# First layer's experts: gather evictions after both halves' matmuls, slot matrices a pair ahead, another order in the last pair's second product

## The chip, the cores and the metric

The program runs on 1 core of one Trainium2 chip, as one launch. The metric is the device time of that core in microseconds (us), the median of several runs. Engine names are those of the profile: PE is TensorE (PEld its weight loads), DVE is VectorE, ACT is ScalarE, POOL is GpSimd, SP is SyncE, which here only issues DMAs.

## What is computed

Two blocks, one after the other, on 512 latent tokens and 256 context tokens of width 1024. The first block has two layers: a mixer (a state-space scan in layer 0, attention in layer 1), then a mixture of experts in which each of 16 experts picks its own tokens. The change lies in layer 0's experts, which serve both token sets:

```python
def moe_ec(h, router_w, w1, w3, w2):
    cap = EC_CAPACITY * T // N_EXPERTS          # 64 latent, 32 context tokens an expert
    aff = jax.nn.softmax(einsum('btd,de->bte', h, router_w))
    gate, idx = lax.top_k(jnp.swapaxes(aff, 1, 2), cap)
    xg = h[bidx, idx]
    a = jnp.einsum('becd,edf->becf', xg, w1)
    g = jnp.einsum('becd,edf->becf', xg, w3)
    y = jnp.einsum('becf,efd->becd', jax.nn.silu(a) * g, w2)
    y = y * gate[..., None]
    return jnp.zeros_like(h).at[bidx, idx].add(y)
```

The second block (convolution, recurrence, pooling, sparse attention, memory attention, a gated feed-forward) follows and isn't touched.

## The kernel before, in words

`Kern.moe` (lines 1073 to 1186) does layer 0's experts, two at a time: 8 pairs. `big` is the latent set (residual `xT`), `small` the context set (residual `cT`). For a pair it forms `moe_w1` and `moe_w3` products (`pa`, `ca` and `pg`, `cg`), takes silu(a)·g on ACT and DVE, turns the three results with transposes (`flip`, banks `tp`), and forms the `moe_w2` product (`py`, `cy`). In a product the selected tokens are the stationary side and 1 MB weight tiles (`wm`, and `raw` in halves) stream past; `cy`, the context part, is interleaved with `py`, the latent part: 24 steps of four matmuls. Weights come through a ring of nine tiles (`Ring`), issued by SP in order as tiles come free.

The **gather**, `Router.quad` (line 328), makes the selected rows `xg` of four latent experts (eight context ones) as one-hot matmuls: for each of 4 PSUM banks, two halves of 8 matmuls (`xrh`, `xrl` over 4 token tiles), and behind each half its eviction, on DVE (line 349) for the first and on ACT (line 347) for the second. `gates` (line 351) follows with 16 small matmuls. Layer 0 gathers before pair 0 (banks `x`, `c`) and, in pairs 1, 3 and 5, after the flips (banks `s`). The same `quad` is called for the context set (lines 682 and 957) and for layer 1's experts (lines 1066 and 1206).

The **scatter** adds pair `pr`'s result `last` to the residuals in pair `pr+1`, between flips and `moe_w2`: `slots` makes one-hot slot matrices (`sp` matmul into PSUM, then `is_equal` on DVE: `ohT` for big, two `ohS` for small), `scatter_big` multiplies and adds on DVE (line 1139), `scatter_small` scales on ACT (`scc`, line 1148) and adds on POOL (line 1149). The last pair's scatter stands behind the loop.

What sets the order: within `moe` the order of TensorE's instructions is the program's (`manual_schedule` for PE); those of the other engines, and all outside `moe`, are put in order at build time by a planner that works with its own time estimates. Each engine then runs its list in order. Dependencies inside PSUM are kept by whole banks: while one engine reads a bank, no other instruction on it starts. Tags name banks through `Slots.MAP` (line 95): `x` is 6, 7; `s` rotates over 6, 0, 7, 1; `a` is 0, 1; `c` is 4, 5; `g` is 2, 3.

Behind `moe`, `attention` starts on the finished residuals: `rms_pe` squares the eight tiles of `xT` on ACT (`sq`, two buffers) and sums them on PE (`rmsps`); ACT makes `rs`; then the products with the first three weight tiles begin, which ACT casts (`whi`, line 443) and POOL splits (`wlo`, line 444).

Of the kernel before, what the change touches and what calls it, by code (L numbers as in the profile page):

```python
# [14 lines left out]
F32R = mybir.dt.float32r  # L15
BF16 = mybir.dt.bfloat16
AF = mybir.ActivationFunctionType
ALU = mybir.AluOpType
# [4 lines left out]
P = 128  # L23
D = 1024
KT = 8
S = 512
C = 256
# [181 lines left out]
class Router:  # L209
# [118 lines left out]
    def quad(self, q, pp, *tags):  # L328

        K, nc, nt, cap, ne = self.K, self.K.nc, self.nt, self.cap, self.ne  # L330
        oh = self.oh = self.rp.tile([P, nt, 256], F32R, name=self.nm + "oh", tag="oh", bufs=1)
        for t in range(nt):
            nc.vector.tensor_tensor(oh[:, t, :].rearrange("p (e j) -> p e j", e=ne),
                                    K.mk["iof"][:, 0:cap].unsqueeze(1).to_broadcast([P, ne, cap]),
                                    self.slot[:, t, q * ne:(q + 1) * ne].unsqueeze(2).to_broadcast([P, ne, cap]), op=ALU.is_equal)
        xg = self.xg[q] = self.xgp.tile([P, KT, 256], F32, name=self.nm + "xg", tag=self.nm + "xg", bufs=self.nq)
        for k2 in range(KT // 2):
            ps = pp.tile([P, 2, 256], F32, name="gth", tag=tags[k2 % len(tags)])
            for z2 in range(2):
                k = 2 * k2 + z2  # L340
                for t in range(nt):
                    for z, r in enumerate((self.rh, self.rl)):
                        nc.tensor.matmul(ps[:, z2, :], r[:, t, k * P:(k + 1) * P], oh[:, t, :],  # L343
                                         start=(t == 0 and z == 0), stop=(t == nt - 1 and z == 1))
                A, sh = K.A2[self.layer][:, self.c, k:k + 1], K.mod(self.layer, 3, self.c, k)
                if z2:
                    nc.scalar.activation(xg[:, k, :], ps[:, z2, :], AF.Identity, scale=A, bias=sh)
                else:
                    nc.vector.tensor_scalar(xg[:, k, :], ps[:, z2, :], A, sh, op0=ALU.mult, op1=ALU.add)
# [28 lines left out]
class Kern:  # L378
# [694 lines left out]
    def moe(self, st, layer, R, nw2):  # L1073
# [3 lines left out]
        nc, tc = self.nc, self.tc  # L1077
        ep = self.pool(st, "moe_e")
        big, small = R
# [4 lines left out]
        ring = Ring(self, rings, 3)  # L1084
        pp = self.pp
        sel, iop = self.mk["sel"], self.mk["iop"]
        bank = lambda nm, tag: pp.tile([P, 512], F32, name=nm, tag=tag)

        def product(nm, pr, lb, ls, pb, pc):

            for q in range(4):
                w = [ring.tile(self.I[nm][layer, 2 * pr + e, q * 256:(q + 1) * 256, :]) for e in range(2)]
                steps = [(a, z) for a in range(2) for z in (0, 1, 2)] if q < 3 else [(a, z) for z in (0, 1, 2) for a in range(2)]
                for a, z in steps:
                    k = 2 * q + a
                    f = dict(start=(k == 0), stop=(k == KT - 1))
                    for e in range(2):
                        for h in range(2):
                            o = 64 * e + 32 * h
                            if z < 2:  # L1100
                                nc.tensor.matmul(pb[z][o:o + 32, :], lb(k, e)[:, 32 * h:32 * h + 32], w[e][a][:, z * 512:(z + 1) * 512], tile_position=(0, o), **f)  # L1101
                            else:
                                nc.tensor.matmul(pc[o:o + 32, :], ls(k, e), w[e][a][:, h * 512:(h + 1) * 512], tile_position=(0, o), **f)  # L1103

        def silu(src):
            t = ep.tile([P, 512], F32, name="ac", tag="ac", bufs=3)
# [1 line left out]
            return t  # L1108

        def flip(src, dst):  # L1110
            tp = bank("tp", "x")
            for j in range(4):
                nc.tensor.transpose(tp[:, j * P:(j + 1) * P], src[:, j * P:(j + 1) * P], self.ident)
            nc.scalar.copy(dst[:, 0:2, :].rearrange("p a b -> p (a b)"), tp[:, 0:256])
            nc.vector.tensor_copy(dst[:, 2:4, :].rearrange("p a b -> p (a b)"), tp[:, 256:512])

        def scaled(src, gate):
            hi = ep.tile([P, 512], F32R, name="yhi", tag="yhi", bufs=3)
            lo = ep.tile([P, 512], F32R, name="ylo", tag="ylo", bufs=3)
            nc.scalar.activation(hi, src, AF.Copy, scale=gate)  # L1120
            nc.vector.scalar_tensor_tensor(lo, src, gate, hi.bitcast(F32), op0=ALU.mult, op1=ALU.subtract)
            return hi, lo

        def slots(s, pr, cols):
            n = s.n
            ps = bank("sp", "s")
            nc.tensor.matmul(ps[:, 0:n], sel[:, pr].rearrange("p e j -> p (e j)"), s.slotT, start=True, stop=True)
            r = []
            for cix in cols:
                t = ep.tile([P, 512], F32R, name="ohT", tag="ohT", bufs=2)[:, 0:n] if n == S else ep.tile([P, C], F32R, name="ohS", tag="ohS", bufs=2)  # L1130
                nc.vector.tensor_scalar(t, ps[:, 0:n], iop[:, cix:cix + 1], None, op0=ALU.is_equal)
                r.append(t)
            return r

        def scatter_big(y, o, k, kk):
            ps = bank("sc", "s")
            for z in range(2):
                nc.tensor.matmul(ps, y[z][:, kk * P:(kk + 1) * P], o, start=(z == 0), stop=(z == 1))
            nc.vector.scalar_tensor_tensor(big.res[:, k, :], ps, self.mod(layer, 5, 0, k), big.res[:, k, :], op0=ALU.mult, op1=ALU.add)

        def scatter_small(y, o, k, kk):
            ps = bank("scs", "s")
            for j in range(2):
                for z in range(2):
                    nc.tensor.matmul(ps[:, j * C:(j + 1) * C], y[z][:, (kk + j) * P:(kk + j + 1) * P], o, start=(j == 0 and z == 0), stop=(j == 1 and z == 1))
            for j in range(2):
                t = ep.tile([P, C], F32, name="scc", tag="scc", bufs=2)
                nc.scalar.activation(t, ps[:, j * C:(j + 1) * C], AF.Copy, scale=self.mod(layer, 5, 1, k + j))  # L1148
                nc.gpsimd.tensor_tensor(small.res[:, k + j, :], small.res[:, k + j, :], t, op=ALU.add)  # L1149

        def scatter(pr, yb, yc):

            ob, oc = slots(big, pr, (0,))[0], slots(small, pr, (1, 2))
            for i in range(4):
                for j in range(2):
                    k = 2 * i + j
                    scatter_big(yb[k // 4], ob, k, k % 4)
                scatter_small(yc, oc[i // 2], 2 * i, 2 * (i % 2))

        with tc.manual_schedule(engines={mybir.EngineType.PE}):  # L1160
            big.quad(0, pp, "x", "c")
            big.gates(0, pp, "x")
            last = None
            for pr in range(8):
                e0 = 2 * pr
                pa, ca = [bank("pa", "a") for _ in range(2)], bank("ca", "c")
                product("moe_w1", pr, lambda k, e: big.rows(k, e0 + e), lambda k, e: small.rows(k, e0 + e), pa, ca)
                ac = [silu(t) for t in (*pa, ca)]
                pg, cg = [bank("pg", "g") for _ in range(2)], bank("cg", "c")
                product("moe_w3", pr, lambda k, e: big.rows(k, e0 + e), lambda k, e: small.rows(k, e0 + e), pg, cg)  # L1170
                for t, g in zip(ac, (*pg, cg)):
                    nc.vector.tensor_tensor(t, t, g, op=ALU.mult)  # L1172
                aT = ep.tile([P, KT, P], F32, name="aT", tag="aT", bufs=1)
                cT = ep.tile([P, 4, P], F32, name="cT", tag="cT", bufs=1)
                for t, o in zip(ac, (aT[:, 0:4, :], aT[:, 4:8, :], cT)):
                    flip(t, o)
                if pr % 2 and pr < 7:
                    big.quad(pr // 2 + 1, pp, "s")
                    big.gates(pr // 2 + 1, pp, "s")
                if last:  # L1180
                    scatter(*last)
                py, cy = [bank("py", "g") for _ in range(2)], bank("cy", "c")
                product("moe_w2", pr, lambda k, e: aT[:, k, 64 * e:64 * e + 64],
                        lambda k, e: cT[:, k % 4, 64 * e + 32 * (k // 4):64 * e + 32 * (k // 4) + 32], py, cy)
                last = (pr, [scaled(t, big.gate[:, pr:pr + 1]) for t in py], scaled(cy, small.gate[:, pr:pr + 1]))
            scatter(*last)

    def moe_last(self, st, R, head):

# [1263 lines left out]
```

## Time and profile before

| | us |
|---|---|
| median of 3 runs | 3378.2 |
| the three runs | 3374.7, 3378.2, 3380.14 |
| the profiled execution | 3374.78 |
| its span | 3373.1 |
| PE / DVE / ACT / POOL busy in the span | 94% / 49% / 35% / 29% |
| mean granted TensorE clock | 0.975 |

Layer 0's experts take about 932 to 1574 us of the span. The times of the sum below are those of the profiled execution, which ran 3.4 us under the median. A granted clock of 1.00 is TensorE's 2.4 GHz, 0.50 its 1.2 GHz.

### The profile page before, as it was taken

What the parts mean: (1) busy time and instruction counts of PE and PEld (TensorE: products, weight loads), DVE (VectorE), ACT (ScalarE), POOL (GpSimd) and SP (SyncE); (2) the same over time, 40 slices, a digit from 0 to 9 for tenths busy, and PEclk for the clock granted to TensorE, in tenths of its full rate; (3) what the DMA queues carried; (4) which work ended last, traced back from release to release, by engine and by line L of the source; (5) the groups of instructions that cost most, each with busy time, mean ns of one, the idle gap of its engine ahead of it and who ended that gap; (6) DMA issues with size and microseconds to landing.
All of it is one profiled execution on the core that took longest, in us unless ns stands there. A gap on an engine that the chain in (4) does not pass through costs nothing.

```text
span 3373.1 us, 47879 instructions
## 1 busy us (share of the span) xinstructions
PE 3160.7 (94%) x18944; PEld 2070.1 (61%) x18944; DVE 1642.3 (49%) x3006; ACT 1169.9 (35%) x2071; POOL 971.8 (29%) x702
## 2 busy tenths in 40 slices
PE   7999989989999999998999999998999999999998
PEld 4677777777734343434667644332367777888886
DVE  5588888886511121113466411014369863763322
ACT  4344444456311111113566400001145354673322
POOL 1354555444200000002602200000054443135543
PEclk9999999999999999999999999999999999999999
DMA  7455333354397979793252579999942224443332
GB/s 248 135 168 166 126 97 91 95 190 150 122 359 281 355 301 358 289 361 131 81 171 74 219 292 409 409 393 344 329 157 66 84 70 135 141 151 106 100 91 85
DMA packets 254097, 668.61 MB, mean 198 GB/s; under 512 B 19312, under 2 KB 73456, under 8 KB 252848
## 3 DMA queue, kind: packets, MB, share of 16 engines
q1 hardware_dynamic: 243920, 645.42, 53.6%
q10 hardware_dynamic: 9952, 20.12, 1.8%
q8 instruction: 149, 2.44, 0.3%
q14 instruction: 76, 0.62, 0.1%
HBM read 651.65 MB, written 13.83 MB: 197 GB/s over the span
## 4 chain that ended last, share of the span: by engine, by line
PE 58%; DVE 8%; DMA 4%; ACT 2%; issue 2%; POOL 1%; SPq 0%; DVEq 0%; POOLq 0%; ACTq 0%
PE mm L473 6%; PE mm L475 6%; PE mm L474 6%; PE py L1320 3%; PE py L1101 3%; PE pa L1101 3%; PE pg L1101 3%; DMA wm<-in_moe_w_dram 3%; PE pa L1242 2%; PE gth L343 2%; PE pg L1242 2%; PE cy L1103 2%; PE ca L1103 2%; PE cg L1103 2%; PE pv L1536 1%
## 5 line engine op out<-in xcount | busy, mean ns | idle before, releaser
L444 POOL TENSOR_TENSOR wlo<-raw,whi 128x1024 fp32r<-128x1024 f32 (+3 forms) x207 | 461.9, 2233 | 662.1 <-ACT whi L443 625.8
L443 ACT CAST whi<-raw 128x1024 fp32r<-128x1024 f32 (+2 forms) x291 | 285.9, 984 | 487.6 <-PE mm L474 206.8
L473 PE MATMUL mm<-stk,whi 128*128 128x512 f32 (+2 forms) x944 | 343.3, 364 | 0.0
L475 PE MATMUL mm<-stk,wlo 128*128 128x512 f32 (+2 forms) x944 | 336.8, 357 | 0.0
L474 PE MATMUL mm<-stk,whi 128*128 128x512 f32 (+2 forms) x944 | 335.5, 355 | 0.0
L473 PE MATMUL pin<-hhi,whi 128*128 128x256 f32 (+1 forms) x768 | 270.1, 352 | 5.2 <-DVE acc L811 4.0
L475 PE MATMUL pin<-hhi,wlo 128*128 128x256 f32 (+1 forms) x768 | 265.0, 345 | 0.0
L474 PE MATMUL pin<-hlo,whi 128*128 128x256 f32 (+1 forms) x768 | 262.8, 342 | 0.0
L1149 POOL TENSOR_TENSOR cT<-cT,scc 128x256 f32<-128x256 f32 x64 | 46.0, 748 | 575.0 <-ACT scc L1148 574.6
L473 PEld LDWEIGHTS mm<-stk,whi 128*128 128x128 f32 (+1 forms) x944 | 180.6, 191 | 32.8 <-issue 7.9
L58 POOL TENSOR_TENSOR sqa<-sqa,sq 128x256 f32<-128x256 f32 (+1 forms) x56 | 64.8, 1157 | 467.9 <-DVE acc L204 411.0
L474 PEld LDWEIGHTS mm<-stk,whi 128*128 128x128 f32 (+1 forms) x944 | 180.4, 191 | 30.2 <-issue 6.2
L475 PEld LDWEIGHTS mm<-stk,wlo 128*128 128x128 f32 (+1 forms) x944 | 179.8, 191 | 26.1 <-issue 1.1
L473 PEld LDWEIGHTS pin<-hhi,whi 128*128 128x128 f32 x768 | 145.7, 190 | 46.2 <-issue 21.7
L474 PEld LDWEIGHTS pin<-hlo,whi 128*128 128x128 f32 x768 | 146.1, 190 | 19.8 <-DVE hlo L600 2.7
L475 PEld LDWEIGHTS pin<-hhi,wlo 128*128 128x128 f32 x768 | 146.0, 190 | 18.2 <-issue 1.7
L1172 DVE TENSOR_TENSOR ac<-ac,pg 128x512 f32<-128x512 f32 x16 | 11.0, 687 | 298.8 <-PE pg L1101 298.8
L811 DVE SCALAR_TENSOR_TENSOR acc<-pin,cwh,acc 128x511 f32<-128x511 f32 (+3 forms) x256 | 148.4, 607 | 14.0 <-ACT acc L806 12.3
L865 DVE SCALAR_TENSOR_TENSOR m<-ab,acum,m 128x128 f32<-128x128 f32 x192 | 118.2, 658 | 23.7 <-POOL m L863 23.7
L1274 DVE TENSOR_TENSOR ac<-ac,pg 128x512 f32<-128x512 f32 x16 | 11.0, 686 | 243.3 <-PE pg L1242 243.3
L444 DVE TENSOR_TENSOR wlo<-raw,whi 128x1024 fp32r<-128x1024 f32 (+1 forms) x84 | 104.7, 1250 | 47.4 <-ACT whi L443 46.6
L1242 PE MATMUL pa<-wm,xxg 128*64 128x512 f32 x416 | 112.6, 597 | 1.9 <-DMA wm<-in_moe_w_dram 1.9
(715 smaller groups left out, 7192.3 us busy)
## 6 DMA issues: line engine op xcount, KB each, us to landing
wm<-in_moe_w_dram SPq DMA_DIRECT2D x255, 1024.0 KB, 9.1
raw<-in_moe_w_dram SPq DMA_DIRECT2D x258, 512.0 KB, 8.6
raw<-in_ada_w_dram SPq DMA_DIRECT2D x96, 512.0 KB, 4.8
raw<-in_w_f_dram SPq DMA_DIRECT2D x68, 512.0 KB, 3.6
raw<-in_w_ssd_in_dram SPq DMA_DIRECT2D x48, 512.0 KB, 4.6
ab<-aS SPq DMA_DIRECT2D x96, 256.0 KB, 4.7
raw<-in_w_in_dram SPq DMA_DIRECT2D x33, 512.0 KB, 3.7
raw<-in_w_ssd_out_dram SPq DMA_DIRECT2D x32, 512.0 KB, 4.1
```

What stands on the lines that cost most here:

```text
L343: nc.tensor.matmul(ps[:, z2, :], r[:, t, k * P:(k + 1) * P], oh[:, t, :], start=(t == 0 and z == 0), stop=(t == nt - 1 and z == 1))
L443: nc.scalar.copy(hi[:, 0:n], raw[:, 0:n])
L444: (eng or self.lo).tensor_tensor(lo[:, 0:n], raw[:, 0:n], hi[:, 0:n].bitcast(F32), op=ALU.subtract)
L473: nc.tensor.matmul(ps, wh, ah, start=start, stop=False)
L474: nc.tensor.matmul(ps, wh, al, start=False, stop=False)
L475: nc.tensor.matmul(ps, wl, ah, start=False, stop=stop)
L811: nc.vector.scalar_tensor_tensor(o, p_[:, lo + s:hi + s], tap(j), o, op0=ALU.mult, op1=ALU.add)
L865: nc.vector.scalar_tensor_tensor(m[:, r, :], ab[:, r, :], acum[:, c, 4 * g + r:4 * g + r + 1], m[:, r, :], op0=ALU.subtract, op1=ALU.min)
L1101: nc.tensor.matmul(pb[z][o:o + 32, :], lb(k, e)[:, 32 * h:32 * h + 32], w[e][a][:, z * 512:(z + 1) * 512], tile_position=(0, o), **f)
L1103: nc.tensor.matmul(pc[o:o + 32, :], ls(k, e), w[e][a][:, h * 512:(h + 1) * 512], tile_position=(0, o), **f)
L1242: nc.tensor.matmul(pb[hf][64 * e:64 * e + 64, :], lb(k, e), w[e][a][:, hf * 512:(hf + 1) * 512], tile_position=(0, 64 * e), **f)
L1320: nc.tensor.matmul(py[half][64 * e:64 * e + 64, :], yb(k, e), w[e][a], start=(k == 0), stop=(k == KT - 1), tile_position=(0, 64 * e))
```

## The change

Four edits. In `quad` the two evictions of a bank stand behind both halves' matmuls. In `flip` the transposes go to the four banks `s`, not the two banks `x`. `slots` of a pair is called just before that pair's `moe_w2` product, and its result kept until the scatter one pair later (`ohS` gets four buffers). In pair 7 `moe_w2` runs all its `py` steps first, then half of the `cy` steps, then scales `py` and scatters it (`big_last`), then the other `cy` steps; the context scatter behind it adds on DVE straight from PSUM, with neither ACT nor POOL.

```diff
                         nc.tensor.matmul(ps[:, z2, :], r[:, t, k * P:(k + 1) * P], oh[:, t, :],
                                          start=(t == 0 and z == 0), stop=(t == nt - 1 and z == 1))
+            for z2 in range(2):
+                k = 2 * k2 + z2
                 A, sh = K.A2[self.layer][:, self.c, k:k + 1], K.mod(self.layer, 3, self.c, k)
                 if z2:
                     nc.scalar.activation(xg[:, k, :], ps[:, z2, :], AF.Identity, scale=A, bias=sh)
...
-        def product(nm, pr, lb, ls, pb, pc):
+        def product(nm, pr, lb, ls, pb, pc, between=None):
+            tiles, late = [], []
+            def step(k, z):
...
             for q in range(4):
...
+                    if between and z == 2:
+                        late.append(k)
+                    else:
+                        step(k, z)
+            for i, k in enumerate(late):
+                if i == len(late) // 2:
+                    between()
+                step(k, 2)
...
-            tp = bank("tp", "x")
+            tp = bank("tp", "s")
...
+        def scatter_small(y, o, k, kk, last=False):
...
+                if last:
+                    nc.vector.scalar_tensor_tensor(r, ps[:, j * C:(j + 1) * C], g, r, op0=ALU.mult, op1=ALU.add)
+                    continue
...
-            ob, oc = slots(big, pr, (0,))[0], slots(small, pr, (1, 2))
...
                 if last:
                     scatter(*last)
+
+                ob, oc = slots(big, pr, (0,))[0], slots(small, pr, (1, 2))
...
+                def big_last():
+                    yb = [scaled(t, gate) for t in py]
+                    for k in range(KT):
+                        scatter_big(yb[k // 4], ob, k, k % 4)
...
-            scatter(*last)
+            yc = scaled(cy, small.gate[:, 7:8])
+            for i in range(4):
+                scatter_small(yc, oc[i // 2], 2 * i, 2 * (i % 2), True)
```

## Rows read from the trace of the kernel before

**Rows 1.** Stretches: start:end, length, busy PE, PEld, DVE, ACT, POOL, clock, DMA, GB/s.

```profile
1010.00:1099.00 89.00, 84.18 (x714) 37.51 (x710) 18.33 (x31) 10.83 (x22) 6.04 (x8) 0.96 0.73 288
2030.00:2110.00 80.00, 79.16 (x394) 34.82 (x394) 10.73 (x26) 6.89 (x14) 0.00 (x0) 1.00 1.03 409
```

**Rows 2.** Timeline, one gather half to the next: start, length, engine, line, [idle before].

```profile
1063.20 0.54 DVE L349 TENSOR_SCALAR xxg<-gth,A,mods 128x256 f32<-128x256 f32 x1 [2.26 <-PE gth L343]
...
1063.80 0.39 PE L343 MATMUL gth<-xoh,xrh 128*128 128x256 f32 x1 [0.64 <-DVE xxg L349]
1064.02 0.28 PE L343 MATMUL gth<-xoh,xrl 128*128 128x256 f32 x1
1064.14 0.28 PE L343 MATMUL gth<-xoh,xrh 128*128 128x256 f32 x1
```

**Rows 3.** Timeline, the same gather some microseconds earlier.

```profile
1058.45 0.41 PE L343 MATMUL gth<-xoh,xrh 128*128 128x256 f32 x1
```

**Rows 4.** Timeline of TensorE in pair 1: third turn, then each stage's first instruction.

```profile
1053.35 0.66 PE L1113 MATMUL tp<-ident,ac 128*128 128x128 f32 x4 [0.48 <-DVE aT L1115]
...
1054.93 0.39 PE L343 MATMUL gth<-xoh,xrh 128*128 128x256 f32 x1 [0.92 <-DVE cT L1115]
...
1067.66 0.17 PE L360 MATMUL pg<-xah,xoh 128*128 128x16 f32 x1
...
1069.44 0.38 PE L1127 MATMUL sp<-xslotT,sel 16*128 16x512 bf16 x1
...
1078.10 1.92 PE L1101 MATMUL py<-wm,aT 128*32 128x512 f32 x16
```

**Rows 5.** Timeline of TensorE in pair 2: first instruction of each stage.

```profile
1140.04 1.09 PE L1113 MATMUL tp<-ident,ac 128*128 128x128 f32 x8
...
1142.20 0.39 PE L1127 MATMUL sp<-xslotT,sel 16*128 16x512 bf16 x1
...
1143.43 0.50 PE L1138 MATMUL sc<-ohT,yhi 128*128 128x512 f32 x1 [0.73 <-DVE ohT L1131]
...
1149.36 1.92 PE L1101 MATMUL py<-wm,aT 128*32 128x512 f32 x16
...
1169.98 1.47 PE L1101 MATMUL pa<-wm,xxg 128*32 128x512 f32 x12
```

**Rows 6.** First gather, first product, last second product; weight DMAs and their landing.

```profile
932.85 0.68 PE L343 MATMUL gth<-xoh,xrh 128*128 128x256 f32 x1
...
938.55 2.65 SPq L125 DMA_DIRECT2D wm<-in_moe_w_dram  x5
...
946.33 1.92 PE L1101 MATMUL pa<-wm,xxg 128*32 128x512 f32 x16
...
1535.75 1.50 PE L1101 MATMUL py<-wm,aT 128*32 128x512 f32 x12
...
DMA to landing us min/median/max: 4.8/8.1/14.6
```

**Rows 7.** Timeline and chain behind the last product: all engines.

```profile
1555.63 0.75 DVE L1121 SCALAR_TENSOR_TENSOR ylo<-py,xgate,yhi 128x512 fp32r<-128x512 f32 x1 [0.97 <-ACT yhi L1120]
...
1557.21 2.93 ACT L443 CAST whi<-raw 128x1024 fp32r<-128x1024 f32 x3
...
1560.69 2.39 POOL wlo L444
...
1567.83 0.80 PE L1138 MATMUL sc<-ohT,yhi 128*128 128x512 f32 x1 [5.23 <-ACT scc L1148]
...
1574.40 1.22 PE L1368 MATMUL rmsps<-sq,ones 128*128 128x512 f32 x1 [3.64 <-ACT sq L1366]
...
1585.32 0.69 ACT L516 ACTIVATE rs<-rmsps,eps 128x512 f32<-128x512 f32 x1 [0.91 <-PE rmsps L1368]
```

**Rows 8.** Timeline, layer 1's first gather.

```profile
1946.88 9.45 PE L343 MATMUL gth<-xoh,stk 128*128 128x256 f32 x56 [1.73 <-DVE xoh L333]
```

**Rows 9.** Timeline, evictions of two flip banks in pair 1.

```profile
1052.87 0.86 DVE L1115 COPY aT<-tp 128x256 f32<-128x256 f32 x2 [0.18 <-ACT aT L1114]
```

More of the change, by code (lines that the diff above doesn't have):

```diff
@@ L1087, in moe @@
         bank = lambda nm, tag: pp.tile([P, 512], F32, name=nm, tag=tag)
-        def product(nm, pr, lb, ls, pb, pc):
-            for q in range(4):
[L1092 to L1103, printed above, removed]
+        def product(nm, pr, lb, ls, pb, pc, between=None):
+            tiles, late = [], []
+            def step(k, z):
+                w, f = tiles[k // 2], dict(start=(k == 0), stop=(k == KT - 1))
+                for e in range(2):
+                    for h in range(2):
+                        o = 64 * e + 32 * h
+                        if z < 2:
+                            nc.tensor.matmul(pb[z][o:o + 32, :], lb(k, e)[:, 32 * h:32 * h + 32], w[e][k % 2][:, z * 512:(z + 1) * 512], tile_position=(0, o), **f)
+                        else:
+                            nc.tensor.matmul(pc[o:o + 32, :], ls(k, e), w[e][k % 2][:, h * 512:(h + 1) * 512], tile_position=(0, o), **f)
+            for q in range(4):
+                tiles.append([ring.tile(self.I[nm][layer, 2 * pr + e, q * 256:(q + 1) * 256, :]) for e in range(2)])
+                for k, z in [(2 * q + a, z) for a in range(2) for z in (0, 1, 2)] if q < 3 else [(2 * q + a, z) for z in (0, 1, 2) for a in range(2)]:
+                    if between and z == 2:
+                        late.append(k)
+                    else:
+                        step(k, z)
[3 more added lines that the diff above has]
+                step(k, 2)
         def silu(src):
@@ L1129, in slots @@
             for cix in cols:
-                t = ep.tile([P, 512], F32R, name="ohT", tag="ohT", bufs=2)[:, 0:n] if n == S else ep.tile([P, C], F32R, name="ohS", tag="ohS", bufs=2)
+                t = ep.tile([P, 512], F32R, name="ohT", tag="ohT", bufs=2)[:, 0:n] if n == S else ep.tile([P, C], F32R, name="ohS", tag="ohS", bufs=4)
                 nc.vector.tensor_scalar(t, ps[:, 0:n], iop[:, cix:cix + 1], None, op0=ALU.is_equal)
@@ L1139, in scatter_big @@
             nc.vector.scalar_tensor_tensor(big.res[:, k, :], ps, self.mod(layer, 5, 0, k), big.res[:, k, :], op0=ALU.mult, op1=ALU.add)
-        def scatter_small(y, o, k, kk):
+        def scatter_small(y, o, k, kk, last=False):
             ps = bank("scs", "s")
@@ L1146, in scatter_small, with scatter @@
             for j in range(2):
+                g, r = self.mod(layer, 5, 1, k + j), small.res[:, k + j, :]
+                if last:
+                    nc.vector.scalar_tensor_tensor(r, ps[:, j * C:(j + 1) * C], g, r, op0=ALU.mult, op1=ALU.add)
+                    continue
                 t = ep.tile([P, C], F32, name="scc", tag="scc", bufs=2)
-                nc.scalar.activation(t, ps[:, j * C:(j + 1) * C], AF.Copy, scale=self.mod(layer, 5, 1, k + j))
-                nc.gpsimd.tensor_tensor(small.res[:, k + j, :], small.res[:, k + j, :], t, op=ALU.add)
-        def scatter(pr, yb, yc):
-            ob, oc = slots(big, pr, (0,))[0], slots(small, pr, (1, 2))
+                nc.scalar.activation(t, ps[:, j * C:(j + 1) * C], AF.Copy, scale=g)
+                nc.gpsimd.tensor_tensor(r, r, t, op=ALU.add)
+        def scatter(yb, yc, ob, oc):
             for i in range(4):
@@ L1181, in moe @@
                     scatter(*last)
+                ob, oc = slots(big, pr, (0,))[0], slots(small, pr, (1, 2))
                 py, cy = [bank("py", "g") for _ in range(2)], bank("cy", "c")
-                product("moe_w2", pr, lambda k, e: aT[:, k, 64 * e:64 * e + 64],
-                        lambda k, e: cT[:, k % 4, 64 * e + 32 * (k // 4):64 * e + 32 * (k // 4) + 32], py, cy)
-                last = (pr, [scaled(t, big.gate[:, pr:pr + 1]) for t in py], scaled(cy, small.gate[:, pr:pr + 1]))
-            scatter(*last)
+                gate = big.gate[:, pr:pr + 1]
+                def big_last():
+                    yb = [scaled(t, gate) for t in py]
+                    for k in range(KT):
+                        scatter_big(yb[k // 4], ob, k, k % 4)
+                product("moe_w2", pr, lambda k, e: aT[:, k, 64 * e:64 * e + 64],
+                        lambda k, e: cT[:, k % 4, 64 * e + 32 * (k // 4):64 * e + 32 * (k // 4) + 32], py, cy, big_last if pr == 7 else None)
+                if pr < 7:
+                    last = ([scaled(t, gate) for t in py], scaled(cy, small.gate[:, pr:pr + 1]), ob, oc)
+            yc = scaled(cy, small.gate[:, 7:8])
+            for i in range(4):
+                scatter_small(yc, oc[i // 2], 2 * i, 2 * (i % 2), True)
     def moe_last(self, st, R, head):
```

## The prediction

> **What bounds the kernel now.** I read the stretches first. While layer 0's experts run, TensorE is busy nearly all the time and the DMA share, near 1.0 inside products, falls to a mean of 0.73 over a stretch with a gather in it [rows 1]: the weight stream has room there, TensorE has none. Its order is the program's, so each wait of it moves the end. In layer 1 it is the reverse: 80 us at 409 GB/s with the DMA share at 1.03 [rows 1], so TensorE time saved in those pairs is given back to the weights; only what moves the start of that stream counts. Then I read TensorE's timeline stage by stage. In a gather the second half of a bank starts only when DVE has read the first: eviction of 0.54 us, TensorE idle for 0.64 us, the first matmul again slow [rows 2]. Earlier in the same gather a matmul takes 0.41 us [rows 3] where its like takes 0.28 [rows 2]: the stretch has a mean granted clock of 0.96 [rows 1], so TensorE fell to 1.2 GHz there, after idle times of 0.48 and 0.92 us [rows 4] and one of the 0.64 us kind. The last reading is the end of the stage: one scatter matmul waited 5.23 us for ACT's `scc`, whose buffers wait for POOL, and POOL had been doing 2.39 us weight splits for attention; `rms_pe` starts only at 1574.40 [rows 7].
>
> **Between products, pairs 0 to 7.** From the first `moe_w1` to the last `moe_w2`, 946.33 to 1535.75 [rows 6], are 589.4 us with 23 products. A product takes 20.62 (1149.36 to 1169.98) [rows 5]; `moe_w3` has 0.1 more behind it, which stays. 589.4 - 23 x 20.62 - 0.8 leaves 114.3 us for flips, gathers, slots and scatters. The same by stage after the change:
>
> Flip: 2.16 us before (1140.04 to 1142.20) [rows 5]. The third turn waits 0.48 for a bank of `x` to be read [rows 4]; with four banks it doesn't, its data being ready by then: 1.66.
>
> Gather: 64 matmuls at 0.12 (starts at 1064.02 and 1064.14) [rows 2]. I take 7.7 us, where pair 1 took 12.73 (1054.93 to 1067.66) [rows 4]. What is late next is the eviction: each bank now has two to evict. I put them one behind the other, since DVE's copy of one half of a flip bank waited for ACT's copy of the other [rows 9]: twice 0.54 [rows 2] and a hand-over, some 1.2 us (an estimate), under the 1.9 us in which the next bank is filled. `s` gives the gather four banks, `x` with `c` as well, so none of this stands in TensorE's way; were the cover gone (two banks), it would be at most 0.3 us a bank.
>
> The Trainium skill (PSUM — Partial Sum Buffer, "PSUM bank collisions raise a hardware error") says that ScalarE and VectorE reading one bank collide too, so they have to be kept apart. This speaks against putting both evictions behind the bank; the trace agrees with the rule by the 0.18 us wait on ACT [rows 9]. By it the pair costs 1.2 us a bank; if the two could overlap, 0.6; the sum is the same by both, as either lies under 1.9.
>
> Gates: 1.78 (1067.66 to 1069.44) [rows 4], unchanged.
>
> Slots: 1.23 before (1142.20 to 1143.43) [rows 5], most of it the wait for `ohT`. The two `sp` matmuls stay on TensorE, now ahead of `moe_w2`: 0.4. They add one wait: a bank of `s`, and the whole product is queued behind it. The first takes the bank of the last scatter's third context tile, the second that of a latent tile; ACT and DVE read both within the scatter's own pace, so 0 to 0.3 a pair. I take 0. `is_equal` on DVE lies beside the product of 20 us; without that cover it costs the 0.8 us of today.
>
> Scatter: 5.93 (1143.43 to 1149.36) [rows 5]; in pair 1 slots and scatter together took 8.66 (1069.44 to 1078.10) [rows 4], against 7.16 in pair 2: the clock again. I take 5.93 for all.
>
> Sum: pair 0 1.66 + 0.4; pairs 1, 3, 5 1.66 + 7.7 + 1.78 + 0.4 + 5.93 = 17.5 each; pairs 2, 4, 6, 7 8.0 each. That is 2.1 + 52.4 + 32.0 = 86.5. **Gain 27.8 us.**
>
> **First gather.** 932.85 to 946.33 is 13.5 us with the gates [rows 6]; after it 7.7 + 0.5 (the slow first matmul) + 1.8 = 10.0, so the first product could start at 942.9. Its second weight tile is issued at 938.55 and the quickest lands 4.8 us later, 943.35 [rows 6]; this doesn't move with the gather. **Gain 2.9**, not 3.5.
>
> **The end.** Count from the start of the last `moe_w2`. Before: `rms_pe` at 1574.40 - 1535.75 = 38.65 [rows 6, 7]. After: a step is 20.62 / 24 = 0.86. 16 `py` steps 13.7; four `cy` steps to 17.2, which hide `yhi` and `ylo` (0.7 + 0.75 [rows 7], done by 15.4); the latent half of the scatter at two thirds of 5.93, 4.0, to 21.2; four `cy` steps to 24.6, which hide the rest of DVE's adds; then scaling `cy` with no cover, 1.6, and the context half, 2.0, to 28.2. ACT has `yhi` and then, since attention's weight buffers lie where the expert weights were, three casts of together 2.93 us [rows 7] before `sq`: 28.5 for the first `sq`, 29.2 for the first matmul. **Gain 9.5.** ACT's and POOL's eight `scc` pairs are gone; DVE's eight context adds (0.4 to 0.75 each, by rows of half and of full width [rows 2, 7]) are wanted only behind the squares of `xT`, 8 us later: nothing. The moved work also moves DMAs: weight tiles of the last product stay until their `cy` step, so SP issues attention's first tiles up to 9 us later in that product. They are cast at 25, so they still have 4 us or more; if one is late ACT stops in front of `sq`, 0 to 4 us. I take 0.
>
> From there `rms_pe` took 10.9 us to `rs` (1574.40 to 1585.32) [rows 7], its first matmul 1.22 long after an idle time of 3.64. At full clock eight squares at 0.86 and a table load on ACT are some 8.5. **Gain 2.4** (0 to 3.5).
>
> **Other callers of the gather.** Layer 1's first gather already runs 56 matmuls in 9.45 us [rows 8]: the planner mixes halves of different banks. I take 1 us there (0 to 3), nothing from its later gathers (weights bound them), 0 +- 1 for the context gathers.
>
> **Sum.** 27.8 + 2.9 + 9.5 + 2.4 + 1 = 43.6. 3374.8 - 43.6 = 3331.2 for an execution like the profiled one, which stands 3.4 under the median of the runs shown: **3334.6**.
>
> **Rivals.** (1) *The end or the clock gives only part.* If a cast or split in front of `sq` takes 5 of the 9.5 us, the slow clock stays in the three pairs with a gather (2 us each) and in `rms_pe` (2.4), 13 us are lost, with all of the 9.5 gone 18: 3348 to 3353. For it: these queues are the planner's. Against: POOL has nothing left that `sq` waits for. (2) *The weight stream takes it back.* Inside products TensorE eats 8.4 MB in 20.6 us, 407 GB/s, as much as DMA moved at its best [rows 1]; if the ring ran dry once gaps shrink, the 27.8 would shrink to about 10: 3352. Against: the share of 0.73 leaves 24 us idle in 89 and only some 9 are taken from such a stretch. (3) *It does nothing*: if evictions still stood between the halves, or the planner's new order elsewhere lost as much: 3372 to 3385. The diff leaves no eviction there. (4) *Slower: the new wait before `moe_w2`.* TensorE's order is fixed, and `sp` needs a bank that ACT frees behind POOL's adds. Where POOL did other work first, such a wait cost 5.23 us [rows 7]. If each of seven pairs paid that, 37 us go and about 7 are left; it turns slower from 6.2 us a pair. At 7.5 us a pair: 3387. Against: inside the loop POOL has only these adds.
>
> **How the numbers follow.** Forecast 0.78, rival 1 0.10, rival 2 0.05, no effect 0.03, slower 0.04. The likeliest case gives 3334.6, its bounds 3330 (1.1 more from the end's clock, 2 more in layer 1, 1 in the context gathers) and 3344 (4 lost to a late tile, 2 to the `sp` bank, 2.4 to the clock, 1 in the context gathers). For 8 in 10 the range reaches into rival 1 and, below, leaves 5 us for the stages that the planner orders anew: 3325 to 3351. 0.2%, some 7 us, is about what a measurement of this kernel can tell from no change; faster by more 0.93, within 0.03, slower 0.04.
>
> **What would show it.** Right: gather banks of 16 matmuls without DVE behind them, under 8 us a gather; no wait for `ohT`; clock 1.00 in the stretch of pair 1; a last `moe_w2` start to first `rmsps` of about 29 us, with no `scc` wait. Wrong: a wait of `sp` for ACT, TensorE waiting for `wm` in products, or `sq` behind a cast that waits for DMA.

## The result and the profile after

| | us |
|---|---|
| median before, 4 runs on that chip | 3376.45 |
| median after, 4 runs (3327.59 to 3335.19) | 3331.85 |
| ratio, 95% interval | 0.9873 [0.9854, 0.9891] |
| the profiled execution after, its span | 3335.19, 3333.5 |
| forecast, range | 3334.6, 3325 to 3351 |

The change makes the kernel 44.6 us faster; 43.6 were forecast. First the two stretches that were changed, on the new kernel: columns as in [rows 1], the upper line the 89 us around pair 1, the lower one from the last `moe_w2` to attention.

```profile
1020.00:1109.00 89.00, 89.00 (x798) 37.29 (x794) 16.53 (x30) 10.89 (x21) 5.65 (x8) 1.00 0.84 329
1507.00:1555.00 48.00, 44.33 (x285) 19.75 (x283) 20.57 (x36) 19.67 (x35) 16.24 (x19) 1.00 0.41 137
```

TensorE is now busy in all 89 us, where it was 84.18; the granted clock is 1.00 where it was 0.96, and the DMA share rises from 0.73 to 0.84 [rows 1]: the weight stream gave more and was not short. TensorE's timeline in pair 1, first instruction of each stage (`flip`, gather, gates, scatter, slots, product; columns: start, length, engine, line, count), against [rows 4]:

```profile
1057.59 1.63 PE L1126 MATMUL tp<-ident,ac 128*128 128x128 f32 x12
...
1058.98 0.36 PE L343 MATMUL gth<-xoh,xrh 128*128 128x256 f32 x1
...
1066.73 0.17 PE L362 MATMUL pg<-xah,xoh 128*128 128x16 f32 x1
...
1068.44 0.48 PE L1151 MATMUL sc<-ohT,yhi 128*128 128x512 f32 x1
...
1074.38 0.38 PE L1140 MATMUL sp<-xslotT,sel 16*128 16x512 bf16 x1
1074.60 0.27 PE L1140 MATMUL sp<-cslotT,sel 16*128 16x256 bf16 x1
1074.80 1.92 PE L1102 MATMUL py<-wm,aT 128*32 128x512 f32 x16
```

Not one of these lines has a bracket: TensorE waits for nobody. The gather takes 7.75 us (1058.98 to 1066.73) for 12.73, `sp` 0.42, the scatter 5.94. What the evictions of a bank do meanwhile, all engines:

```profile
1063.09 0.54 DVE L351 TENSOR_SCALAR xxg<-gth,A,mods 128x256 f32<-128x256 f32 x1 [1.38 <-PE gth L343]
...
1063.67 0.56 ACT L349 ACTIVATE xxg<-gth,mods,A 128x256 f32<-128x256 f32 x1 [1.35 <-DVE xxg L351]
...
1065.01 0.54 DVE L351 TENSOR_SCALAR xxg<-gth,A,mods 128x256 f32<-128x256 f32 x1 [1.38 <-PE gth L343]
...
1065.59 0.57 ACT L349 ACTIVATE xxg<-gth,mods,A 128x256 f32<-128x256 f32 x1 [1.36 <-DVE xxg L351]
```

The bank is full before 1063.09, yet ACT starts at 1063.67, 0.04 us behind DVE's end: one after the other, 1.14 us of the 1.92 from bank to bank. The Trainium skill (PSUM — Partial Sum Buffer, "PSUM bank collisions raise a hardware error") asks that ScalarE and VectorE never read one bank in the same partitions at once, whichever of its columns each reads; the trace agrees, with those 0.04 us between them. The end of the stage, all engines, against [rows 6, 7]:

```profile
1511.99 3.64 PE L1102 MATMUL py<-wm,aT 128*32 128x512 f32 x32
...
1537.81 2.94 ACT L445 CAST whi<-raw 128x1024 fp32r<-128x1024 f32 x3
...
1537.97 0.38 PE L1158 MATMUL scs<-ohS,yhi 128*128 128x256 f32 x1 [0.81 <-ACT yhi L1133]
...
1538.75 0.39 PE L1158 MATMUL scs<-ohS,ylo 128*128 128x256 f32 x1 [0.40 <-DVE ylo L1134]
...
1540.90 0.63 ACT L1394 ACTIVATE sq<-xT 128x512 f32<-128x512 f32 x1 [0.15 <-issue]
...
1541.58 6.66 PE L1396 MATMUL rmsps<-sq,ones 128*128 128x512 f32 x14 [0.77 <-ACT sq L1394]
...
1550.22 0.69 ACT L518 ACTIVATE rs<-rmsps,eps 128x512 f32<-128x512 f32 x1 [0.91 <-PE rmsps L1396]
```

`rmsps` starts 29.59 us after the last `moe_w2` (1511.99 to 1541.58), against 38.65, and `rs` 8.64 us later, against 10.92. No `sc` waits for `scc`.

**Where the 39.6 us between the two profiled spans went**, from the starts of stages in both timelines:

| stretch | before | after | gain | forecast |
|---|---|---|---|---|
| start to the first gather | 932.85 | 939.98 | -7.1 | 0 |
| first gather to first `flip` | 54.82 | 53.74 | 1.1 | 2.9 |
| first `flip` to last `moe_w2` | 548.08 | 518.27 | 29.8 | 27.8 |
| last `moe_w2` to `rmsps` | 38.65 | 29.59 | 9.1 | 9.5 |
| `rmsps` to attention's first product | 14.03 | 11.75 | 2.3 | 2.4 |
| from there to the end | 1784.7 | 1780.2 | 4.5 | 1 |

The 29.8 us by stage: flips 17.97 to 11.18 (6.8), three gathers 35.39 to 23.27 (12.1), slots 10.37 to 3.36 (7.0), scatters 45.44 to 41.75 (3.7), gates 0.2. The lost 7.1 us of the first line lie in the first 940 us, where each engine has the same list of instructions in both kernels up to the context gather. It starts at 796.77 us before and at 803.86 after, so the 7.1 us are lost ahead of it; e10 below shows that they belong to the execution.

### The profile page after: what moved, and what is told of

It is laid out like the page before. It is cut to its first block, busy times and chain, and to the rows that moved or that the text cites. A ratio compares the mean times of both kernels' runs of the same rounds, so it can differ in the third digit from the quotient of the medians.

```text
span 3333.5 us, 47840 instructions
## 1 busy us (share of the span) xinstructions
PE 3143.5 (94%) x18944; PEld 2061.6 (62%) x18944; DVE 1644.7 (49%) x3014; ACT 1165.3 (35%) x2063; POOL 963.3 (29%) x694
## 4 chain that ended last, share of the span: by engine, by line
PE 60%; DVE 9%; DMA 4%; ACT 2%; issue 2%; POOL 1%; SPq 0%; DVEq 0%; ACTq 0%; POOLq 0%
PE mm L475 6%; PE mm L477 6%; PE mm L476 6%; PE py L1348 4%; PE py L1102 3%; PE pg L1102 3%; PE pa L1102 3%; PE pa L1270 3%; DMA wm<-in_moe_w_dram 3%; PE pg L1270 2%; PE gth L343 2%; PE cy L1104 2%; PE cg L1104 2%; PE ca L1104 2%; PE pv L1564 1%
## 5 line engine op out<-in xcount | busy, mean ns | idle before, releaser
L1166 POOL TENSOR_TENSOR cT<-cT,scc 128x256 f32<-128x256 f32 x56 | 39.6, 736 | 545.4 <-ACT scc L1165 544.9
L872 POOL TENSOR_TENSOR ce<-ce,xc 128x1024 f32<-128x1024 f32 (+1 forms) x48 | 103.4, 2155 | 39.6 <-ACT ce L871 39.5
```

The costliest lines, as they stand in the source:

```text
L872: nc.gpsimd.tensor_tensor(ce[:, j0:j1, :], ce[:, j0:j1, :], conv["C"][:, o:o + P].unsqueeze(1).to_broadcast([P, j1 - j0, P]), op=ALU.mult)
```

## The experiments

A stage's time below is always from its first instruction to the first of the next, on TensorE's timeline of that run.

**e1, the gather alone.** The kernel before, with this in `quad`:

```diff
                                          start=(t == 0 and z == 0), stop=(t == nt - 1 and z == 1))
+            for z2 in range(2):
+                k = 2 * k2 + z2
```

> Only the gather edit, on the kernel before. Theory (the eviction between the halves idles TensorE, and the idle time also costs clock): the three gathers in the loop go from 12.7, 11.3 and 11.4 us to about 7.8 each, the first from 11.7 to about 8.1, with 2 us of that returned as a wait for weights in the first product; slots and scatter of pairs 1, 3 and 5 go from 8.5 to 8.7 us to about 7.2, since the gather in front no longer leaves TensorE at the lower clock. In all 16 to 19 us less. Rival (the lower clock in those scatters comes from their own wait for the slot matrices): they stay at 8.5 us or more, in all 12 to 14 us less.

3355.79 us, ratio 0.9944 [0.9929, 0.9959] to 3372.91 before. TensorE in pair 1:

```profile
1051.17 0.39 PE L343 MATMUL gth<-xoh,xrh 128*128 128x256 f32 x1 [0.92 <-DVE cT L1117]
...
1060.72 0.38 PE L1129 MATMUL sp<-xslotT,sel 16*128 16x512 bf16 x1
...
1062.08 0.47 PE L1140 MATMUL sc<-ohT,yhi 128*128 128x512 f32 x1 [0.87 <-DVE ohT L1133]
...
1064.48 0.63 PE L1140 MATMUL sc<-ohT,ylo 128*128 128x512 f32 x1
```

The gather takes 7.77, 7.74 and 7.77 us in pairs 1, 3 and 5, with the flips as slow as ever. But the scatters behind them still take 7.33, 7.31 and 7.31: they begin at full clock (0.47), stand at 0.63 two microseconds after the 0.87 us wait for `ohT`, and recover later. So the slow clock there isn't the gather's, and by the stages it is the rival that holds: from the first gather to attention's first product they give 13.0 us, although the median's 17.1 would fit the theory.

**e2, the flips alone**: `tp = bank("tp", "s")` in the kernel before.

> Only the flips' banks, on the kernel before. Theory (the third turn waits for a bank): each of the eight flips goes from 2.0 to 2.2 us to 1.4 to 1.7, 4 to 6 us less in all. Rival (the data of the third turn is what comes last): under 1 us in all.

3370.38, ratio 0.9985 [0.9973, 0.9996]. TensorE in pair 1:

```profile
1052.65 1.63 PE L1113 MATMUL tp<-ident,ac 128*128 128x128 f32 x12
...
1055.86 0.39 PE L343 MATMUL gth<-xoh,xrh 128*128 128x256 f32 x1 [0.64 <-DVE xxg L349]
...
1068.47 0.47 PE L1138 MATMUL sc<-ohT,yhi 128*128 128x512 f32 x1 [0.87 <-DVE ohT L1131]
```

The twelve transposes run as one group, 1.38 us to the gather; the eight flips take 11.9 us instead of 18.0, more than the median shows. The gather, with its 0.64 us waits, falls from 12.73 to 11.30: in this pair its slow clock goes with the waits of 0.48 and 0.92 us ahead of it [rows 4]. They aren't enough by themselves, though: e1 keeps both, takes away only the 0.64 us waits, and its gather runs at full clock too. The scatter stays at 7.30, and in pairs 3 and 5 it takes 7.82 and 8.01, more than the 7.31 and 7.16 before: there the clock falls already among the gates' matmuls, ahead of the wait for `ohT`.

**e3, the slot matrices alone**, in the kernel before:

```diff
-            ob, oc = slots(big, pr, (0,))[0], slots(small, pr, (1, 2))
...
+                ob, oc = slots(big, pr, (0,))[0], slots(small, pr, (1, 2))
                 py, cy = [bank("py", "g") for _ in range(2)], bank("cy", "c")
```

> Only the slot matrices made before the second product, on the kernel before. Theory (TensorE waits for is_equal on DVE): from the end of flip or gates to the start of the second product 6.3 us instead of 7.2 to 7.7 in pairs 2, 4, 6 and 7 and 6.3 to 7.5 instead of 8.5 to 8.7 in pairs 1, 3 and 5, 6 to 10 us less in all. Rival (the sp matmul now waits for a bank that ACT frees behind POOL, with the product queued behind it): a wait of 1 us or more at sp in every pair, and no gain.

3364.35, ratio 0.9975 [0.9965, 0.9984]. Slots take 0.43 us and `sp` waits for no bank. Flips, still in two banks, take 2.0 us, and 3.15 in pairs 4 and 5, where the 0.48 and 0.92 us waits meet. The scatters take 5.95 and 5.87 us in pairs 3 and 5, with gathers as slow as before (11.3); pair 1 still has 7.28, its clock falling with the last of the gates. So in two of the three pairs the slow scatter went with the wait for `ohT`; in the third it came without that wait. Pair 5 adds a row on the gather: it has the two waits ahead of the gather that pair 1 of the kernel before has [rows 4], and the 0.64 us waits in it, but stays at full clock. Its timeline, and the stretch of the gather in the kernel before (pair 1) and here (pair 5), columns as in [rows 1]:

```profile
1363.86 0.66 PE L1113 MATMUL tp<-ident,ac 128*128 128x128 f32 x4 [0.49 <-DVE aT L1115]
...
1365.44 0.38 PE L343 MATMUL gth<-xoh,xrh 128*128 128x256 f32 x1 [0.92 <-DVE cT L1115]
```

```profile
1054.93:1067.66 12.73, 10.18 (x65) 9.27 (x65) 2.17 (x4) 1.70 (x3) 0.00 (x0) 0.87 0.44 174
```

```profile
1365.44:1376.80 11.36, 8.80 (x65) 8.00 (x66) 2.18 (x4) 1.69 (x3) 0.00 (x0) 1.00 0.48 191
```

With e1, no single edit gives full clock in all three pairs; the three together do (5.94, 5.93, 5.87).

**e4, the last pair alone**: `between`, `big_last` and `last=True` in the kernel before, with its `slots` still behind the scatter in pairs 0 to 6.

> Only the last pair's second product and its scatter, on the kernel before. Theory (attention's start waits for POOL's adds behind its weight splits): from the start of the last second product to the first sum of squares 29 to 30 us instead of 38.7, and that sum to rs 8.6 instead of 10.9; 11 to 12 us less in all. Rival (attention's weights, now loaded later, come last): the casts wait for DMA and half of it is lost, 5 to 7 us less.

3358.17, ratio 0.9954 [0.9939, 0.9969]. From the last `moe_w2` to `rmsps` 29.58 us, from there to attention's first product 11.75: the end of the full change, alone. Medians of e1 to e4 lie 17.1, 2.5, 8.6 and 14.7 us under the same 3372.91, together 43.0; all at once gave 44.6. Each of these medians is uncertain by 3 to 5 us; by the stages from the first gather to attention's first product the four give 13.0, 6.6, 10.2 and 10.9, together 40.7, and all at once 42.2. So the parts add up to within 2 us, with no large gain that hides behind another.

**e5, the last context adds over ACT and POOL.** The changed kernel with one flag less:

```diff
-                scatter_small(yc, oc[i // 2], 2 * i, 2 * (i % 2), True)
+                scatter_small(yc, oc[i // 2], 2 * i, 2 * (i % 2))
```

> The changed kernel, but the last context adds go over ACT and POOL as they did before. It tells the new order in the last second product from the engine of the adds. Theory (POOL's adds were what attention waited for): from the start of that product to the first sum of squares 33 to 38 us instead of 29.6, since the squares stand behind eight scalings that wait for eight adds of 0.74 us. Rival (the order alone brings it): 29 to 31 us.

3342.62, ratio 0.9900 [0.9885, 0.9915]. ACT, POOL and TensorE at the end:

```profile
1530.00 2.65 POOL L1439 MEMSET kB<- 64x3072 f32 x1 [25.09 <-issue]
1532.73 1.40 POOL L1166 TENSOR_TENSOR cT<-cT,scc 128x256 f32<-128x256 f32 x2
1534.10 2.34 POOL L446 TENSOR_TENSOR wlo<-raw,whi 128x1024 fp32r<-128x1024 f32 x1
1536.39 1.40 POOL L1166 TENSOR_TENSOR cT<-cT,scc 128x256 f32<-128x256 f32 x2
...
1545.14 0.63 ACT L1394 ACTIVATE sq<-xT 128x512 f32<-128x512 f32 x1 [3.18 <-POOL cT L1166]
...
1545.82 2.93 PE L1396 MATMUL rmsps<-sq,ones 128*128 128x512 f32 x3 [13.82 <-ACT sq L1394]
```

42.63 us from the last `moe_w2` (1503.19) to `rmsps`: 13 more than with the adds on DVE, outside the 33 to 38 expected and even above the 38.65 of the kernel before. POOL's list alternates two adds (1.40) with a weight split of attention (2.34), behind a memset of 2.65, and ACT's first square stands behind all of it. The other order of the product is worth nothing without the small edit that takes the last adds off POOL and their scalings off ACT. The reverse wasn't run: what that small edit would give in the old order, and so what the new order adds to it, isn't shown.

**e6, other callers.** The changed kernel, in which all gathers but the latent ones of layer 0 evict each half at once, as before:

```diff
+                if not (self.layer == 0 and self.c == 0):
+                    self.evict(xg, ps, k, z2)
+            if self.layer == 0 and self.c == 0:
+                for z2 in range(2):
+                    self.evict(xg, ps, 2 * k2 + z2, z2)
```

> The changed kernel, but the evictions behind both halves only in layer 0's latent gathers; the context gathers and layer 1's as before. Theory (the planner had mixed the halves there, and weights bound layer 1): 0 to 3 us slower than the changed kernel, within what can be measured; layer 1's first gather takes 1 us longer to its first product. Rival (the other callers carry a good part): 5 us or more slower.

3326.27, ratio 0.9858 [0.9844, 0.9873], 5.6 us under the changed kernel's 3331.85 with intervals that overlap. Layer 1's first gather, here and then in the changed kernel:

```profile
1902.83 9.37 PE L343 MATMUL gth<-xoh,stk 128*128 128x256 f32 x56 [1.73 <-DVE xoh L333]
1912.13 1.07 PE L1276 MATMUL pa<-wm,xxg 128*64 128x512 f32 x2
...
1914.27 1.94 PE L1276 MATMUL pa<-wm,xxg 128*64 128x512 f32 x8
```

```profile
1908.70 10.90 PE L343 MATMUL gth<-xoh,stk 128*128 128x256 f32 x64 [1.73 <-DVE xoh L333]
1919.54 1.94 PE L1270 MATMUL pa<-wm,xxg 128*64 128x512 f32 x8
```

With evictions per half the planner lets eight of the 64 matmuls run after the first two of the product, which begin 9.3 us after the gather's start; the product goes on at 11.4. In the changed kernel all 64 come first, and the product runs from 10.8 on. Neither is clearly ahead, and the 1 us forecast from other callers isn't there.

**e7, the latent scatter behind all `cy` steps** of the changed kernel:

```diff
-                if i == len(late) // 2:
-                    between()
                 step(k, 2)
+            if between:
+                between()
```

> The changed kernel, but the latent scatter of the last pair stands behind all context steps, not half of them, so that it covers the scaling of cy. Theory (1.0 us and the casts are all that is left in front of the squares): from the start of the product to the first sum of squares 27 to 28 us instead of 29.6, 1.5 to 2.5 us less. Rival (the squares' space is free only behind the last scatter, or DVE's latent adds, now later, come last): 29 us or more, no gain.

3329.93, ratio 0.9871 [0.9856, 0.9885]. DVE and TensorE at the end:

```profile
1524.50 5.36 DVE L1152 SCALAR_TENSOR_TENSOR xT<-sc,mods,xT 128x512 f32<-128x512 f32 x8 [6.02 <-PE sc L1151]
1529.78 0.74 DVE L1134 SCALAR_TENSOR_TENSOR ylo<-cy,cgate,yhi 128x512 fp32r<-128x512 f32 x1
...
1530.57 0.39 PE L1158 MATMUL scs<-ohS,ylo 128*128 128x256 f32 x1 [2.19 <-DVE ylo L1134]
...
1532.25 0.41 PE L1158 MATMUL scs<-ohS,ylo 128*128 128x256 f32 x1
...
1534.29 2.07 PE L1396 MATMUL rmsps<-sq,ones 128*128 128x512 f32 x2 [0.77 <-ACT sq L1394]
```

31.29 us instead of the 27 to 28 expected. The scaling of `cy` was to hide beside the scatter; but its DVE half (`ylo`) went into DVE's list behind the eight adds, TensorE waited 2.19 us, and its clock fell (0.28 to 0.41), so that `rmsps` to attention took 13.53 instead of 11.75. The stages lose 3.5 us; the median doesn't show it, which says how little a median of four tells at this size.

**e8, three half tiles early.** The changed kernel with another order of the ring's nine places:

```diff
+        ring.seq = ring.seq[:1] + [None] * 3 + ring.seq[1:6]
```

> The changed kernel, but layer 0's weight ring takes its three half-loaded places second to fourth instead of last. These are loaded before the gather, so the first product should not wait for weights; and they are also last in the last second product, so attention's first weights are loaded only as its last context steps end. Theory: pair 0's first two products 41.4 us instead of 43.9; at the end the casts in front of the squares wait for DMA, and the first sum of squares comes 32 to 34 us behind the product's start instead of 29.6; together 0 to 2 us slower. Rival (late weights for attention are covered anyhow): the end stays at 29.6, 2 to 3 us faster.

3325.5, ratio 0.9853 [0.9834, 0.9871]. In the changed kernel TensorE waits in the first product:

```profile
962.69 1.48 PE L1102 MATMUL pa<-wm,xxg 128*32 128x512 f32 x10 [1.28 <-DMA wm<-in_moe_w_dram]
```

and its first two products take 43.88 us, at 409 GB/s and a DMA share of 1.03. Here, SP's issues and the stretch of the same two products (columns as in [rows 1]):

```profile
916.37 14.88 SPq L130 DMA_DIRECT2D raw<-in_moe_w_dram  x5
935.84 10.09 SPq L125 DMA_DIRECT2D wm<-in_moe_w_dram  x6
945.97 5.54 SPq L130 DMA_DIRECT2D raw<-in_moe_w_dram  x6
```

```profile
940.18:981.52 41.34, 41.34 (x386) 12.40 (x385) 3.12 (x8) 2.66 (x4) 0.00 (x0) 1.00 1.03 410
```

41.34 us, TensorE busy throughout. The stream moves as much per microsecond in both; what differs is that the `raw` tiles, issued ahead of the gather, are now the second to fourth in use, and the `wm` tiles have longer to land. The 2.5 us that the first gather lost again are thus a wait for weights, as forecast in kind. The end is 29.71, not the 32 to 34 of the theory: no late tile holds up `sq`, and the expectation's rival holds. The median lies 6.3 us under the changed kernel's, with intervals that overlap.

**e9 and e10, the two small gains together, beside the changed kernel itself.** e9 is e6 and e8 in one; e10 is the changed kernel, unaltered, on the same chip.

> The changed kernel with two things that runs above showed singly: the gather's evictions moved in the latent gathers of layer 0 alone, and the ring's order w1, three raw, w2 x5. Theory (first product's weight wait of 2.5 us is the ring's; other callers carry nothing): the first two products take 41.4 us instead of 43.9, the rest to the last moe_w2 as in the changed kernel, the end 29.6 us; the time 2 to 6 us under the changed kernel on the same chip, near 3326. Rival (both differences were start-up and execution noise of some 4 us): within 2 us of the changed kernel.

> The changed kernel once more, beside e9 on one chip. Theory: 0.987 of the kernel before, as at first. First flip to last moe_w2 518.3 us again and 29.6 us at the end, within 0.3 us; the start of the first gather anywhere from 930 to 940 us (start-up), and so the time 3325 to 3336. Rival (the late start of 939.98 us belongs to the change): the first gather starts at 938 us or later again.

e9 3330.97, ratio 0.9877 [0.9856, 0.9898]; e10 3329.93, ratio 0.9867 [0.9847, 0.9887]. In e9 no product waits for weights and the first two take 41.34 us, but no gain shows in the time, where some 3326 was expected: that e6 and e8 beat the changed kernel isn't confirmed. e10 repeats the stages from the first flip on within 0.05 us (518.31 us to the last `moe_w2`, 29.57 at the end); from the first gather to the first flip it takes 53.29, for 53.74. Its first gather, though, starts here:

```profile
929.55 0.68 PE L343 MATMUL gth<-xoh,xrh 128*128 128x256 f32 x1
```

10.4 us earlier than in the changed kernel's first profile. In the 14 profiles of this study this start lies anywhere from 929.55 to 939.98, that of the kernel before at 932.85. The 7.1 us in the table above are start-up, not the change.

**e11 and e12, fewer banks.** The changed kernel with the gathers of pairs 1, 3 and 5 in one bank, and in two:

```diff
-    MAP = dict(... c=(4, 5), x=(6, 7), s=(6, 0, 7, 1), ...)
+    MAP = dict(... c=(4, 5), x=(6, 7), q=(2,), s=(6, 0, 7, 1), ...)
...
-                    big.quad(pr // 2 + 1, pp, "s")
+                    big.quad(pr // 2 + 1, pp, "q")
```

(e12: `q=(2, 3)`.)

> The changed kernel with the gathers of pairs 1, 3 and 5 in one PSUM bank instead of four. It takes the cover of the evictions away. Theory (the gain of the gather is that evictions of a bank, 0.54 us on DVE and then 0.56 us on ACT with a hand-over, lie beside the filling of the next): each of three refills waits some 1.4 us, so 7.75 + 4.2 = 12 us a gather, at or above the 11.3 us of the kernel before; if idle times lower the clock, up to 15; 13 to 22 us slower than the changed kernel. Rival (the gain is only in fewer turns between PE and DVE, four instead of seven): 9 to 10 us a gather.

> The changed kernel with the gathers of pairs 1, 3 and 5 in two PSUM banks instead of four. Theory (evictions of a bank take 1.14 us one behind the other and a bank is filled in 1.92 us): no wait, 7.75 us a gather as with four, and the time of the changed kernel. Bound named in the prediction for the cover gone: up to 0.3 us a bank, 8.4 to 9 us a gather. Rival (with two banks each eviction is in the way): 9 us or more.

e11 3344.61, ratio 0.9915 [0.989, 0.9941]; e12 3330.76, ratio 0.9874 [0.9847, 0.9901]. All engines at a refill in e11:

```profile
1059.93 0.54 DVE L351 TENSOR_SCALAR xxg<-gth,A,mods 128x256 f32<-128x256 f32 x1 [1.08 <-PE gth L343]
1060.51 0.56 ACT L349 ACTIVATE xxg<-gth,mods,A 128x256 f32<-128x256 f32 x1 [2.11 <-DVE xxg L351]
1061.13 0.39 PE L343 MATMUL gth<-xoh,xrh 128*128 128x256 f32 x1 [1.24 <-ACT xxg L349]
```

With one bank both evictions stand in TensorE's way and a gather takes 12.22 us, more than the 11.3 of the kernel before at full clock. With two it takes 7.75 to 7.76, as with four. So the gain of the gather needs a second bank and no more, and the 0.3 us a bank that the prediction allowed for "two banks" was not needed: 1.14 us of evictions lie under 1.92 of filling.

## Why the prediction was right

- **What bounds it.** Right: TensorE's order is the program's, and 29.8 us of idle and slow time between products became 29.8 us of span. From the first flip to the last `moe_w2` the list of TensorE's waits is empty, with no weight wait in products 3 to 23; rival 2 falls except for the first product, and rival 3 (no effect) lies outside the interval.
- **Gather**, 7.7 forecast: 7.74 to 7.76 in pairs 1, 3, 5 and 8.08 ahead of pair 0; the two serial evictions were put at 1.2 us and take 1.14 [rows 2, 9].
- **Flips**, 1.66 forecast: 1.38. The step that failed took off only the 0.48 us wait [rows 4] from 2.16 (which is 1.68, not 1.66). The wait also laid bare the tail of the eight transposes ahead of it (1.09) [rows 5] and slowed the four behind it (0.66) [rows 4]; without it all twelve run as one group of 1.63. That is some 2 us more over eight pairs, and nearly all of the gap between 27.8 and 29.8.
- **Slots**, 0.4 forecast without a wait for a bank: 0.42, no wait in any pair. Rival 4, which needed 6.2 us a pair, falls.
- **Scatter**, 5.93 everywhere: 5.87 to 6.15. Right in size, half wrong in cause: the prediction blamed the slow clock on the waits of the flips and of the gather. e1 takes the gather's away and all three scatters stay slow, e3 takes the wait for `ohT` away and two of three are at full clock. Why the third isn't stays open. Had only the gather been changed, 4 us would have been missing from the sum.
- **First gather**, 2.9 forecast, 1.1 measured (1.5 in e10): the mis-sized term. The gather and gates end 3.6 us sooner, and the prediction took off 0.6 for the second weight tile. That part is right. The product starts on the first tile at 949.84; the load that needs the next tile comes 1.06 us later, where the kernel before takes 0.46:

```profile
950.90 0.16 PEld L1102 LDWEIGHTS pa<-wm,xxg 128*32 128x32 f32 x8 [0.92 <-DMA wm<-in_moe_w_dram]
```

What the step left out is a later tile, which costs 1.5 us (1.28 of them idle in one wait, shown with e8), and 0.4 in the last step of the two products, whose four matmuls no longer start together. With the 0.6 these are the 2.5 us that the two products took more. The step looked at the first tile that could be late instead of at the stream, which at a DMA share of 1.03 had no room to catch up. e8 gives the 2.5 us back.

- **The end**, 9.5 forecast, 9.1 measured. The scaling of `cy` without cover costs 0.81 and 0.40 us of waits, the casts stand in front of `sq` for 2.94 as counted [rows 7], and `sq` follows 0.15 us behind them. The clock stays at 1.00, and `rmsps` to `rs` takes 8.64 (8.5 forecast). Rival 1 falls on both counts. e5 shows that the sentence on ACT's and POOL's `scc` pairs can't be done without: with the pairs back the end takes 13 us more.
- **Other callers**, 1 forecast: nothing (e6). The 4.5 us between attention's first product and the end aren't theirs: that stretch took 1776.5 to 1785.7 in the profiles of the changed kernel and its variants, 1777.9 in e10, which is the changed kernel once more, and 1784.7 before. How much of it is the change's stays open.
- **The forecast's closeness** is partly luck. Start-up (10.4 us between two profiles of one kernel) and the stretch behind attention's first product (2.3 us between the same two, 9 over the variants) vary by more than any single error in the sum, and of these errors 2.0 us too little for the flips and 1.8 too much for the first gather cancel.

## What to carry to other kernels

When two engines evict one PSUM bank, put both evictions behind the bank's last matmul and have a second bank to fill meanwhile; compare the evictions' sum (1.14 us) with the fill (1.92 us), since with one bank the same order costs more than it saves. At the seam of two stages, list everything that the planner put on each engine ahead of the instruction you are waiting for: eight adds on POOL cost 13 us because of whose work stood between them. And before a shift of some microseconds is read as an effect, find the first instruction at which two traces differ in time; here it lay long before the first changed one.

## What the runs showed of the hardware that was not expected

An idle time alone doesn't set the clock. In e11 each gather has three waits of 1.24 us, and TensorE stays at 2.4 GHz (matmuls of 0.28 us, a scatter of 5.94). In e1 one wait of 0.87 us, behind the gates' small matmuls of 128x16 and the two `sp` ones, is followed by 1.2 GHz in all three pairs (0.63 for a matmul that takes 0.40), and in pair 2 of the kernel before, where a flip and not the gates came ahead, a wait of 0.73 is not [rows 5]. The row of waits doesn't settle it either: with the same two waits ahead of it and the 0.64 us ones within, the gather of pair 1 in the kernel before has a granted clock of 0.87, that of pair 5 in e3 one of 1.00. And in pairs 3 and 5 of e2 the clock falls among the gates' matmuls, with no wait since the gather's last. What decides, these rows don't show.
